# Smaller first loads, partial sums of two column blocks in one PSUM bank, and new planning estimates in a two-layer encoder trunk

## The chip, the cores and the metric

One Trainium2 chip, one core. The metric is the device time of one execution in microseconds (us), the median of several runs; lower is better. Matrix products run on PE (TensorE) and land in PSUM, which has eight banks of 512 fp32 columns per partition. DVE (VectorE), ACT (ScalarE) and POOL (GpSimd) do the elementwise work, and SP's queue issues nearly all DMAs.

## What is computed

Two layers over 256 tokens of width 1024, all in fp32. Each layer is: half a SwiGLU feed-forward (hidden width 2816), a mixer, cross attention to a memory of 256 tokens, and another half feed-forward. Layer 0's mixer is a differential attention beside a stick-breaking attention with one output projection; layer 1's is multi-head latent attention (MLA) with 16 heads.

```python
for layer in range(DEPTH):
    x = x + 0.5 * swiglu(rms_norm(x, ffn_norm[layer, 0]), w_gate, w_up, w_down)
    h = rms_norm(x, mix_norm[layer])
    x = x + (diff_stickbreak_mixer(h, ...) if layer % 2 == 0 else mla_mixer(h, ...))
    x = x + memory_cross_attention(rms_norm(x, xm_norm[layer]), rms_norm(mem, ...), ...)
    x = x + 0.5 * swiglu(rms_norm(x, ffn_norm[layer, 1]), w_gate, w_up, w_down)
```

## The kernel before

**Arithmetic.** Every fp32 product of weights is made of three matmuls on halves (mm3, L284 to L289): each operand is split into a rounded high part and a remainder, and high x high, low x high and high x low are summed in PSUM. Splitting costs one ACT cast (wh, L250) and one DVE subtraction (wl, L252; in the mixers the last 512 columns of a chunk go to POOL). The activations are kept feature by token (tile x, 8 blocks of 128 features by 256 tokens), also as pairs xh and xl.

**Weights.** They come in chunks of 1 MB in a fixed order (_plan). A chunk has one of two raw buffers (RAW), then one of three buffers of split halves (HL). A call of weight for chunk i issues loads and splits up to chunk i+2 (LOOK). The raw buffer comes free when its chunk is split, the split buffer when PE has used it.

**Start.** Before the first feed-forward, x and the first gate chunk are loaded in four parts each, and then the two halves of the first up chunk, the token-major copy of x (xtok, for the norm) and constants; the norm weights (gains) are loaded by SP's queue as the third DMA (L1483). fm_first runs the first gate chunk as its parts arrive. The norm's factor per token (rs) is computed by four ACT squares (L1497), and spread over the partitions by one matmul (spread) into rb, by which DVE scales the gate and up products when it empties their banks (L705, L713). For the first pair of chunks the PE order is gate 0, up 0, gate 1 with spread in its middle, and then up 1. Products take one of three banks tagged mm.

**PE's order in the mixers.** PE executes in exactly the order in which the program writes its instructions. In the mixers and cross attentions this order is made by a planner (run, L450): tasks are generators that yield what they need (a bank, an event, a chunk, a latency), planned times come from tables (EST_AB, EST_MLA, EST_X0, EST_X1) and from spend, and at each step the task with the lowest priority number of those that are ready goes on. The products and the output projection are one task of the lowest priority, the filler. If a real latency is longer than its estimate, PE stands and waits, with everything behind it. The other engines' orders are chosen by the framework's scheduler, also when the program is built.

**Output projection (out_g, L653).** The output has eight column blocks dt of 128 features. Its sum over the heads comes in groups, one for each event src at which heads are ready (four groups in the mixers, two in the cross attentions); one group of one block is two triples, six matmuls. A window of three blocks, each in its own mm bank, is taken through all groups, and then the other five blocks one by one. At a block's last group finish_dt adds the bank to x (DVE, L510), splits the result (ACT L481, DVE L482), squares it (ACT L522) and adds the square (POOL L530).

**MLA queries (L1312).** For each of 4 groups of heads and 2 halves of the tokens, queries scales the product, squares it, sums, takes one rsqrt (POOL, L467) and rotates in a scratch tile.

Of the kernel before, what the change touches and what calls it, by code (L numbers as in the profile page):

```python
# [53 lines left out]
SLOTS_MLA = (29, 11)  # L54
# [5 lines left out]
EST_X0 = {'scale': 3.59, 'rq': 1.14, 'psd': 1.46, 'sp': 2.8, 'p1': 4.06, 'p2': 0, 'o': 1.32, 'src': 8.83}  # L60
EST_X1 = {'scale': 2.31, 'rq': 1.14, 'psd': 1.46, 'sp': 2.8, 'p1': 3.39, 'p2': 0.0, 'o': 1.18, 'src': 8.83}
EST_AB = {'b': 1.33, 'va': 1.47, 'rot': 14.92, 'st1': 6.44, 'st2': 0.14, 'z': 1.55, 'sto': 2.4, 'src': 0.79, 'T': 0.74, 'sp': 3.0, 'pc': 8.7, 'pcT': 1.4, 'po': 4.35, 'oa': 8.7, 'srco': 1.25}
PRIO_MLA = [1, 2, 4.2, 3.9, 4.4, 2.3]
PRIO_AB = [1, 6.1, 4.1, 6.9, 6.9, 0.5]
EST_MLA = {'latd': 1.52, 'scale': 11.0, 'r': 1.8, 'kr': 4.06, 'pk': 2.4, 'pv': 1.23, 'v': 1.73, 'k': 6.43, 'kT': 0.9, 'q': 7.82, 'qT': 2.38, 'cs': 3.11, 'sp': 6.25, 'p1': 3.36, 'p2': 0.68, 'p3': 0.75, 'o': 0.58, 'src': 0.8}
MLA_ORDER = (('k', 0), ('kv', 0), ('kv', 1), ('q', 0), ('q', 1), ('k', 1), ('q', 2), ('q', 3), ('v', 0))
# [95 lines left out]
def trunk_kernel(ctx, tc, wflat, xT_d, xtok_d, memT_d, memtok_d, gains_d, rows_d, cst_d, out_d):  # L162
# [133 lines left out]
    nc.sync.dma_start(x[:, 0:2, :], xT_d[:, 0:2, :])  # L296
# [10 lines left out]
    for _ in range(13):  # L307
        PE.matmul(pw[:, 0:P], ones, ones, start=True, stop=True)
# [299 lines left out]
    def fm(w, xg, between=None, order=PLAIN):  # L608
        ps = ps_("mm")
# [43 lines left out]
    def out_g(keyf, nchunk, groups, gc):  # L653

        begin_phase()
        per = KT // nchunk
        ws, left, pss = {}, {c: per for c in range(nchunk)}, {}

        def part(dt, g):
            _, src, rows_ = groups[g]  # L660
            w = ws[dt // per]
            j = dt % per
            for i, k in enumerate(rows_):
                mm3(pss[dt][:, 0:S], (w[0][:, k, j * P:(j + 1) * P], w[1][:, k, j * P:(j + 1) * P]),
                    src[i], g == 0 and i == 0, g == len(groups) - 1 and i == len(rows_) - 1)
            if g == len(groups) - 1:
                left[dt // per] -= 1
                if not left[dt // per]:
                    done(keyf(dt // per))
                ps = pss.pop(dt)  # L670
                finish_dt(dt, gc, ps[:, 0:S])
                drop(ps, 0.8)

        nw = BANKS["mm"]
        for win in [tuple(range(nw))] + [(dt,) for dt in range(nw, KT)]:
            for g, (ev, _, _) in enumerate(groups):
                for dt in win:
                    yield dict(after=[ev], w=keyf(dt // per), mm=int(g == 0))
                    if dt // per not in ws:
                        ws[dt // per] = weight(keyf(dt // per), per * P)  # L680
                    if g == 0:
                        pss[dt] = take("mm")
                    part(dt, g)


    def ffn(l, j, gc, need_rb, mem=None):
# [4 lines left out]
        for f in range(FT // 2):  # L691
            pg = (fm_first(xg) if ("gate", l, j, f) == FIRST else
                  ahead or fm(weight(("gate", l, j, f), P), xg, order=PLAIN if f else EARLY))
            ahead = None
            if f == 0:
                if l == j == 0:
# [13 lines left out]
            if f:  # L710
                pu = fm(weight(("up", l, j, f), P), xg)
            u = al()
# [96 lines left out]
    def mem_k(l, c, events):  # L809
# [4 lines left out]
        def norm():  # L814
# [13 lines left out]
            yield dict(t=1, lat=7.0)  # L828
# [371 lines left out]
    def mixer_mla(gc):  # L1200
# [7 lines left out]
        rl, kk, kf, vt, kT, qf, rqs = {}, {}, {}, {}, {}, {}, {}  # L1208
# [88 lines left out]
        def turn_k(hf):  # L1297
            kT[hf] = []
            for g in range(4):
# [7 lines left out]
                drop(pt, 0.9)  # L1307
# [4 lines left out]
        def queries(n, t, ps):  # L1312

            yield dict(after=[ev["rcq"]])
            if t == 0:
                qf[n], rqs[n] = [], sl()
# [21 lines left out]
            rel(sq, tmp)  # L1338
# [137 lines left out]
    with arena(*SLOTS_FFN):  # L1476
        begin_phase()
        for h in range(4):
            if h:
                nc.sync.dma_start(x[:, 2 * h:2 * h + 2, :], xT_d[:, 2 * h:2 * h + 2, :])  # L1480
            split_w = issue_part(0, h, 4)
            if h == 0:
                nc.sync.dma_start(gains[:, 0:NG], gains_d)  # L1483
            for dt in (2 * h, 2 * h + 1):
# [8 lines left out]
        ss = sm()
        for q in range(4):
            xt = al()
            nc.sync.dma_start(xt, xtok_d[:, q // 2, (q % 2) * 512:(q % 2 + 1) * 512])
            A.activation(xt, xt, AF.Square, accum_out=ss[:, q:q + 1])  # L1497
            rel(xt)
        nc.sync.dma_start(cst, cst_d[:, 0:512])
        V.tensor_reduce(out=st.var, in_=ss[:, 0:4].rearrange("p (a b) -> p a b", b=2), axis=AX.X, op=ALU.add)  # L1500
        V.tensor_scalar(out=st.var, in0=st.var, scalar1=1.0 / D, scalar2=EPS, op0=ALU.mult, op1=ALU.add)
        rsqrt(st.var, 2, st.rs)
# [88 lines left out]
```

## Time and profile before

| what | us |
|---|---|
| median of 3 runs | 1087.91 (1087.11 to 1088.03) |
| profiled execution | 1090.49 |
| its span, first to last instruction | 1088.8 |
| PE busy in the span | 1065.9 |
| DVE, ACT, POOL busy | 769.4, 655.4, 192.5 |

The span is what the profile's rows cover. Starts are counted from its beginning. PE's matmuls are pipelined: a 128x256 matmul is shown with 0.28 us, but the next one starts 0.11 us after it, so time lost by PE is read from starts. The granted clock is TensorE's, as a share of 2.4 GHz; its other level is 1.2 GHz.

### The profile page before, as it was taken

What the parts mean: (1) busy time and instruction counts of PE and PEld (TensorE: products, weight loads), DVE (VectorE), ACT (ScalarE), POOL (GpSimd) and SP (SyncE); (2) the same over time, 40 slices, a digit from 0 to 9 for tenths busy, and PEclk for the clock granted to TensorE, in tenths of its full rate; (3) what the DMA queues carried; (4) which work ended last, traced back from release to release, by engine and by line L of the source; (5) the groups of instructions that cost most, each with busy time, mean ns of one, the idle gap of its engine ahead of it and who ended that gap; (6) DMA issues with size and microseconds to landing.
All of it is one profiled execution on the core that took longest, in us unless ns stands there. A gap on an engine that the chain in (4) does not pass through costs nothing.

```text
span 1088.8 us, 23382 instructions
## 1 busy us (share of the span) xinstructions
PE 1065.9 (98%) x9040; PEld 1046.5 (96%) x9040; DVE 769.4 (71%) x1866; ACT 655.4 (60%) x1775; POOL 192.5 (18%) x210
## 2 busy tenths in 40 slices
PE   9999999999989999999999999999989999999998
PEld 8899999998889999999999999999878999999998
DVE  5978766567867877776677777654678768777753
ACT  6666555576756765555565655555867567555542
POOL 1100001356245200000100000014861422000000
PEclk9999999999999999999999999999989999999999
DMA  8765555635346365545556555555342444555561
GB/s 291 248 223 209 195 198 186 195 116 161 111 126 199 107 219 179 211 177 198 185 194 219 193 215 179 202 186 161 110 131 64 144 145 167 205 190 198 184 220 63
DMA packets 50800, 193.36 MB, mean 178 GB/s; under 512 B 5760, under 2 KB 7552, under 8 KB 35584
## 3 DMA queue, kind: packets, MB, share of 16 engines
q1 hardware_dynamic: 50688, 191.86, 51.3%
q8 instruction: 71, 1.16, 0.4%
q14 instruction: 41, 0.34, 0.1%
HBM read 190.79 MB, written 1.05 MB: 176 GB/s over the span
## 4 chain that ended last, share of the span: by engine, by line
PE 87%; DVE 5%; ACT 2%; POOL 2%; DMA 2%; issue 1%; SPq 0%; DVEq 0%; ACTq 0%; POOLq 0%
PE mm L286 28%; PE mm L288 27%; PE mm L287 27%; DVE wl L252 2%; DMA wr<-wflat 2%; ACT slotf L754 1%; PE t L767 1%; POOL sm L467 1%; PE s L1422 1%; PE t L475 1%; PE s L892 0%; PE o L1455 0%; DVE sm L745 0%; ACT wh L250 0%; POOL sl L467 0%
## 5 line engine op out<-in xcount | busy, mean ns | idle before, releaser
L250 ACT CAST wh<-wr 128x256 fp32r<-128x256 f32 (+1 forms) x1216 | 441.2, 434 | 294.9 <-PE mm L287 237.8
L252 DVE TENSOR_TENSOR wl<-wr,wh 128x256 fp32r<-128x256 f32 (+1 forms) x1171 | 479.5, 464 | 122.1 <-ACT wh L250 117.1
L286 PE MATMUL mm<-xh,wh 128*128 128x256 f32 x1584 | 439.9, 278 | 3.8 <-DVE slotf L705 2.6
L288 PE MATMUL mm<-xh,wl 128*128 128x256 f32 x1584 | 437.6, 276 | 0.1
L287 PE MATMUL mm<-xl,wh 128*128 128x256 f32 x1584 | 437.4, 276 | 0.0
L286 PEld LDWEIGHTS mm<-xh,wh 128*128 128x128 f32 x1584 | 298.3, 188 | 5.0 <-issue 2.8
L287 PEld LDWEIGHTS mm<-xl,wh 128*128 128x128 f32 x1584 | 298.4, 188 | 0.6
L288 PEld LDWEIGHTS mm<-xh,wl 128*128 128x128 f32 x1584 | 298.1, 188 | 0.7 <-DVE wl L273 0.4
L286 PE MATMUL mm<-slotr,wh 128*128 128x256 f32 x896 | 247.6, 276 | 0.3 <-ACT slotr L481 0.3
L287 PE MATMUL mm<-slotr,wh 128*128 128x256 f32 x896 | 246.6, 275 | 0.4 <-DVE slotr L482 0.4
L288 PE MATMUL mm<-slotr,wl 128*128 128x256 f32 x896 | 246.5, 275 | 0.0
L286 PEld LDWEIGHTS mm<-slotr,wh 128*128 128x128 f32 x896 | 168.2, 188 | 1.0 <-ACT slotr L481 0.6
L287 PEld LDWEIGHTS mm<-slotr,wh 128*128 128x128 f32 x896 | 168.2, 188 | 0.7 <-DVE slotr L482 0.6
L288 PEld LDWEIGHTS mm<-slotr,wl 128*128 128x128 f32 x896 | 168.2, 188 | 0.0
L530 POOL TENSOR_TENSOR acc<-acc,sq 128x256 f32<-128x256 f32 x49 | 38.7, 790 | 455.0 <-ACT sq L522 452.9
L252 POOL TENSOR_TENSOR wl<-wr,wh 128x512 fp32r<-128x512 f32 x45 | 67.4, 1497 | 110.3 <-ACT wh L250 92.2
L713 DVE TENSOR_TENSOR slotf<-mm,rb 128x512 f32<-128x512 f32 x44 | 30.4, 690 | 59.4 <-PE mm L288 59.4
L481 ACT ACTIVATE xh<-x,gains 128x256 fp32r<-128x256 f32 x64 | 32.1, 507 | 29.8 <-DVE x L510 25.8
L705 DVE TENSOR_TENSOR slotf<-mm,rb 128x512 f32<-128x512 f32 x44 | 30.3, 689 | 23.4 <-PE mm L288 23.2
L754 ACT ACTIVATE slotf<-s,sm,sl 128x256 f32<-128x256 f32 (+1 forms) x64 | 32.8, 522 | 23.3 <-DVE sm L748 17.8
L510 DVE SCALAR_TENSOR_TENSOR x<-mm,x 128x256 f32<-128x256 f32 x64 | 26.7, 418 | 23.5 <-PE mm L288 23.3
L482 DVE SCALAR_TENSOR_TENSOR xl<-x,gains,xh 128x256 fp32r<-128x256 f32 x64 | 37.5, 590 | 5.3 <-ACT xh L481 5.2
(196 smaller groups left out, 1152.7 us busy)
## 6 DMA issues: line engine op xcount, KB each, us to landing
wr<-wflat SPq DMA_DIRECT2D x118, 1024.0 KB, 4.9
wr<-wflat SPq DMA_DIRECT2D x180, 256.0 KB, 3.9
wr<-wflat SPq DMA_DIRECT2D x16, 768.0 KB, 4.2
slotf<-memT SPq DMA_DIRECT2D x8, 256.0 KB, 3.4
x<-xT SPq DMA_DIRECT2D x4, 256.0 KB, 4.9
wr<-wflat SPq DMA_DIRECT2D x2, 512.0 KB, 8.2
slotf<-xtok SPq DMA_DIRECT2D x4, 256.0 KB, 7.8
slotf<-memtok SPq DMA_DIRECT2D x4, 256.0 KB, 3.6
```

The lines of the kernel that those rows point to most:

```text
L250: A.copy(hi[:, a:b], raw[:, a:b])
L252: e.tensor_tensor(out=lo[:, a:b], in0=raw[:, a:b], in1=hi[:, a:b].bitcast(F32), op=ALU.subtract)
L286: PE.matmul(out, a[0], b[0], start=first, stop=False, **kw)
L287: PE.matmul(out, a[0], b[1], start=False, stop=False, **kw)
L288: PE.matmul(out, a[1], b[0], start=False, stop=last, **kw)
L481: return (A.activation(hi, src, AF.Identity, scale=g), V.scalar_tensor_tensor(out=lo, in0=src, scalar=g, in1=hi.bitcast(F32), op0=ALU.mult ...
L482: V.scalar_tensor_tensor(out=lo, in0=src, scalar=g, in1=hi.bitcast(F32), op0=ALU.mult, op1=ALU.subtract))
L510: V.scalar_tensor_tensor(out=xd, in0=ps, scalar=factor, in1=xd, op0=ALU.mult, op1=ALU.add)
L530: G.tensor_tensor(out=st.acc, in0=st.acc, in1=sq, op=ALU.add)
L705: V.tensor_tensor(out=t.rearrange("p (a b) -> p a b", b=S), in0=pg.rearrange("p (a b) -> p a b", b=S), in1=rbb, op=ALU.mult)
L713: V.tensor_tensor(out=u.rearrange("p (a b) -> p a b", b=S), in0=pu.rearrange("p (a b) -> p a b", b=S), in1=rbb, op=ALU.mult)
L754: A.activation(p[:, i * w:(i + 1) * w], sps[:, i * w:(i + 1) * w], AF.Exp, bias=nb[:, i:i + 1], scale=r, accum_out=sums[:, i:i + 1])
```

## The change

1. Start: gains goes out first, by ScalarE's queue. x and the first gate chunk come in five parts (blocks 0, 1, 2-3, 4-5, 6-7). The token-major x and the norm move into first_norm, which the program now writes behind the first gate product; the constants are loaded in two pieces. PE's order is gate 0, up 0, gate 1, up 1 with spread in its middle, then gate 2; up 1 and gate 2 take the two banks tagged s, which the feed-forward doesn't use otherwise. setup (rope tables, masks) moves from the first pair to the fourth. 10 warming matmuls instead of 13.
2. out_g: two blocks share a bank, so the window has six blocks, and then one and one.
3. queries: one rsqrt for both halves of the tokens, scratch inside the tiles at hand, the rotation ahead of the sum.
4. Planner: new estimates, among them va, sp and srco (layer 0), k, kT, q, sp, p1, o and src (MLA), src of the cross attentions, 9 instead of 7 for a memory key; 0.115 instead of 0.109 per matmul; in MLA's product order the second key-value chunk moves behind two query chunks, and the last memory-value chunk ahead of the last query chunk. One more SBUF slot in MLA.

```diff
-EST_AB = {... 'va': 1.47, ... 'sp': 3.0, ... 'srco': 1.25}
+EST_AB = {... 'va': 2.8, ... 'sp': 4.4, ... 'srco': 2.2}
-EST_MLA = {... 'k': 6.43, 'kT': 0.9, 'q': 7.82, 'qT': 2.38, 'cs': 3.11, 'sp': 6.25, 'p1': 3.36, 'p2': 0.68, ... 'o': 0.58, 'src': 0.8}
+EST_MLA = {... 'k': 9.0, 'kT': 1.5, 'q': 8.0, 'qT': 3.0, 'cs': 2.0, 'sp': 4.6, 'p1': 4.4, 'p2': 1.2, ... 'o': 2.2, 'src': 1.6}
-MLA_ORDER = (('k', 0), ('kv', 0), ('kv', 1), ('q', 0), ('q', 1), ('k', 1), ('q', 2), ('q', 3), ('v', 0))
+MLA_ORDER = (('k', 0), ('kv', 0), ('q', 0), ('q', 1), ('kv', 1), ('k', 1), ('q', 2), ('v', 0), ('q', 3))
...
-    nc.sync.dma_start(x[:, 0:2, :], xT_d[:, 0:2, :])
+    nc.scalar.dma_start(gains[:, 0:NG], gains_d)
+    nc.sync.dma_start(x[:, 0:1, :], xT_d[:, 0:1, :])
...
             for i, k in enumerate(rows_):
-                mm3(pss[dt][:, 0:S], (w[0][:, k, j * P:(j + 1) * P], w[1][:, k, j * P:(j + 1) * P]),
-                    src[i], g == 0 and i == 0, g == len(groups) - 1 and i == len(rows_) - 1)
+                mm3(ps[:, dt % 2 * S:dt % 2 * S + S], (w[0][:, k, j * P:(j + 1) * P], w[1][:, k, j * P:(j + 1) * P]),
+                    src[i], g == i == dt % 2 == 0, g == len(groups) - 1 and i == len(rows_) - 1,
+                    skip_group_check=True)
...
-                ps = pss.pop(dt)
-                finish_dt(dt, gc, ps[:, 0:S])
-                drop(ps, 0.8)
+                finish_dt(dt, gc, ps[:, dt % 2 * S:dt % 2 * S + S])
+                if dt % 2:
+                    drop(ps, 0.8)
 
-        nw = BANKS["mm"]
+        nw = 2 * BANKS["mm"]
...
                 if first_:
+                    first_norm()
                     pu = fm(weight(("up", l, j, f), P), xg)
-                    ahead = fm(weight(("gate", l, j, 1), P), xg, tick)
-                    setup()
+                    ahead = (fm(weight(("gate", l, j, 1), P), xg),
+                             fm(weight(("up", l, j, 1), P), xg, tick, tag="s"))
...
+            if t:
+                v = qv[n][:, 0:8]
+                V.tensor_scalar(out=v, in0=v, scalar1=96 * EPS, scalar2=None, op0=ALU.add)
+                rsqrt(v, 8, rqs[n])
```

## Rows read from the trace of the kernel before

**Rows 1.** The page, part 1: busy us (share of the span) x instructions.
```profile
PE 1065.9 (98%) x9040; PEld 1046.5 (96%) x9040; DVE 769.4 (71%) x1866; ACT 655.4 (60%) x1775; POOL 192.5 (18%) x210
```
**Rows 2.** Stretches: length, busy us of each engine, clock, DMA share, GB/s.
```profile
0.00:40.00 40.00, 35.07 (x245) 33.49 (x246) 28.09 (x78) 26.84 (x76) 6.20 (x20) 0.96 0.82 279
...
200.00:273.00 73.00, 71.17 (x607) 68.24 (x605) 47.90 (x74) 47.19 (x102) 39.07 (x39) 1.00 0.47 150
273.00:345.00 72.00, 67.13 (x580) 65.05 (x579) 53.84 (x115) 45.27 (x109) 30.11 (x25) 1.00 0.45 143
345.00:370.00 25.00, 24.43 (x183) 23.07 (x182) 19.60 (x49) 18.08 (x50) 5.22 (x6) 1.00 0.33 122
...
733.00:800.00 67.00, 62.10 (x443) 57.79 (x443) 39.09 (x85) 44.10 (x86) 46.00 (x50) 0.97 0.41 132
800.00:847.00 47.00, 44.98 (x330) 39.95 (x330) 40.72 (x115) 31.95 (x94) 13.01 (x16) 0.97 0.27 87
```
**Rows 3.** Waits of PE over the span: us in total, times, longest.
```profile
PE s L1422 <- DVE slotf L1409: 2.6, 1, 2.6
PE t L767 <- DVE slotf L827: 2.5, 2, 2.2
PE s L323 <- ACT slotf L754: 2.3, 3, 1.0
PE t L767 <- ACT slotf L1305: 1.4, 1, 1.4
...
PE o L1079 <- issue: 0.9, 1, 0.9
PE o L1079 <- ACT slotf L991: 0.9, 1, 0.9
```
**Rows 4.** Timeline of PE, 20 to 32 us: start, us, operation, idle before.
```profile
20.88 0.39 PE L286 MATMUL mm<-xh,wh 128*128 128x256 f32 x1 [1.17 <-ACT wh L250]
...
27.10 0.28 PE L288 MATMUL mm<-xh,wl 128*128 128x256 f32 x1
30.02 0.35 PE L286 MATMUL mm<-xh,wh 128*128 128x256 f32 x1 [2.64 <-DVE slotf L705]
...
31.16 0.41 PE L286 MATMUL mm<-xh,wh 128*128 128x256 f32 x1
```
**Rows 5.** Timeline of SP, ACT and DVE, 6 to 30 us.
```profile
6.78 3.25 SPq L1496 DMA_DIRECT2D slotf<-xtok  x4
...
13.03 3.84 SPq L248 DMA_DIRECT2D wr<-wflat  x2
...
20.42 2.56 ACT L250 CAST wh<-wr 128x256 fp32r<-128x256 f32 x8 [2.04 <-DMA wr<-wflat]
...
24.31 4.03 DVE L252 TENSOR_TENSOR wl<-wr,wh 128x256 fp32r<-128x256 f32 x8 [0.68 <-ACT wh L250]
...
29.19 0.68 DVE L705 TENSOR_TENSOR slotf<-mm,rb 128x512 f32<-128x512 f32 x1
```
**Rows 6.** The POOL rsqrt of L467 in the MLA stage, 773 to 818 us.
```profile
L467 POOL TENSOR_TENSOR sl<-sm,small x7: 1006/1377/1583, 785.9 to 814.6; 128x4 f32<-128x4 f32 x7
```
**Rows 7.** Timeline of ACT, 757 to 761 us.
```profile
757.74 0.60 ACT L1218 ACTIVATE slotf<-mm 128x512 f32<-128x512 f32 x1 [0.46 <-DVE slotr L482]
759.92 0.84 ACT L818 ACTIVATE slotf<-mm,small 128x256 f32<-128x256 f32 x2 [1.58 <-PE mm L288]
```
**Rows 8.** Timeline of PE and DVE, the output projection of layer 0's mixer.
```profile
317.91 0.28 PE L288 MATMUL mm<-slotr,wl 128*128 128x256 f32 x1
...
319.27 0.28 PE L288 MATMUL mm<-slotr,wl 128*128 128x256 f32 x1
...
318.22 0.42 DVE L510 SCALAR_TENSOR_TENSOR x<-mm,x 128x256 f32<-128x256 f32 x1 [2.35 <-PE mm L288]
...
322.67 0.41 DVE L510 SCALAR_TENSOR_TENSOR x<-mm,x 128x256 f32<-128x256 f32 x1
...
333.69 0.41 DVE L510 SCALAR_TENSOR_TENSOR x<-mm,x 128x256 f32<-128x256 f32 x1
```

More of the change, by code (lines that the diff above doesn't have):

```diff
@@ L306, in trunk_kernel @@
     pw = ps_("o")
-    for _ in range(13):
+    for _ in range(10):
         PE.matmul(pw[:, 0:P], ones, ones, start=True, stop=True)
@@ L605, in trunk_kernel, with fm @@
     PLAIN = [(j, k) for j in range(2) for k in range(KT)]
-    def fm(w, xg, between=None, order=PLAIN):
-        ps = ps_("mm")
+    def fm(w, xg, between=None, order=PLAIN, tag="mm"):
+        ps = ps_(tag)
         for j, k in order:
@@ L677, in out_g, with first_norm @@
                 for dt in win:
-                    yield dict(after=[ev], w=keyf(dt // per), mm=int(g == 0))
+                    yield dict(after=[ev], w=keyf(dt // per), mm=int(g == 0 and dt % 2 == 0))
                     if dt // per not in ws:
                         ws[dt // per] = weight(keyf(dt // per), per * P)
-                    if g == 0:
-                        pss[dt] = take("mm")
+                    if g == 0 and dt % 2 == 0:
+                        pss[dt // 2] = take("mm")
                     part(dt, g)
+    def first_norm():
+        ss = sm()
+        for q in range(4):
+            xt = al()
+            nc.sync.dma_start(xt, xtok_d[:, q // 2, (q % 2) * 512:(q % 2 + 1) * 512])
+            A.activation(xt, xt, AF.Square, accum_out=ss[:, q:q + 1])
+            rel(xt)
+        nc.sync.dma_start(ident, cst_d[:, C_ID:C_ID + P])
+        with tc.high_priority():
+            V.tensor_reduce(out=st.var, in_=ss[:, 0:4].rearrange("p (a b) -> p a b", b=2), axis=AX.X, op=ALU.add)
+            V.tensor_scalar(out=st.var, in0=st.var, scalar1=1.0 / D, scalar2=EPS, op0=ALU.mult, op1=ALU.add)
+            rsqrt(st.var, 2, st.rs)
     def ffn(l, j, gc, need_rb, mem=None):
@@ L691, in ffn @@
         for f in range(FT // 2):
[L692 to L693 removed]
+            first_ = l == j == 0
+            pu = None
+            if ahead and f:
+                pg, pu = ahead
+            elif first_ and f == 0:
+                pg = fm_first(xg)
+            else:
+                pg = fm(weight(("gate", l, j, f), P), xg, order=PLAIN if f else EARLY,
+                        tag="s" if first_ and f == 2 else "mm")
             ahead = None
             if f == 0:
[L696 removed]
+                if first_:
+                    first_norm()
                     pu = fm(weight(("up", l, j, f), P), xg)
[L698 to L699 removed]
+                    ahead = (fm(weight(("gate", l, j, 1), P), xg),
+                             fm(weight(("up", l, j, 1), P), xg, tick, tag="s"))
                 else:
@@ L709, in ffn @@
             rel(t)
-            if f:
+            if pu is None:
                 pu = fm(weight(("up", l, j, f), P), xg)
+            if first_ and f == 3:
+                setup()
             u = al()
@@ L1477, in trunk_kernel @@
         begin_phase()
[L1478 to L1484, printed above, removed]
+        for k0, k1 in ((0, 1), (1, 2), (2, 4), (4, 6), (6, 8)):
+            if k0:
+                nc.sync.dma_start(x[:, k0:k1, :], xT_d[:, k0:k1, :])
+            split_w = issue_part(0, k0 * 256, k1 * 256)
+            for dt in range(k0, k1):
                 for made in finish_dt(dt, G_FFN):
@@ L1488, in trunk_kernel @@
         for h in range(2):
-            issue_part(1, h, 2)()
+            issue_part(1, h * 1024, (h + 1) * 1024)()
         st.xg = st.nxt
         st.rs, st.var, st.rb = sl()[:, 0:2], sl()[:, 0:2], T("rb", [P, S], 1)
[L1493 to L1502, printed above, removed]
         st.todo = [spread]
```

40 lines of the change are left out of this document (19 added, 21 removed).

## Prediction

> **What bounds the kernel now.** I read the page's busy times first: PE is busy for 1065.9 of 1088.8 us [rows 1], so the end is PE's work plus PE's waits, and no other engine is near the bound over the span. Then the stretches: PE's idle time sits in the start (40.00 - 35.07 = 4.9 us, 1.1 of it before anything can run), in layer 0's mixer (1.83 + 4.87 = 6.7), in MLA (4.90 + 2.02 = 6.9) and, 0.6 each, in the first cross attention [rows 2] and in the second. The granted clock is below 1 in the start and in MLA. A mean of 0.96 over 40 us, with 0.5 and 1 as the only levels, is 3.2 us at 1.2 GHz, of which half, 1.6 us, is lost; 0.97 over 67 and 47 us loses 2.0 and 1.4 us [rows 2]. In the start the fall follows the 2.64 us wait: from 31.16 us a matmul takes 0.41 us instead of 0.28 [rows 4].
>
> Third, the waits by name [rows 3]: nearly all are PE standing at an instruction whose data is late by 1 to 2.6 us, in an order fixed when the program was written. Idle time understates them. Before the 2.64 us wait PE's starts are 27.10 and 30.02, 2.92 apart instead of 0.11, and the next matmuls start slower: a wait costs about 0.25 us more than its idle row [rows 4]. With some 6 such waits in layer 0's mixer and 10 in MLA, what can be won is about 8.2 us and, with the clock, 6.9 + 2.5 + 3.4 = 12.8 us.
>
> **Start.** PE stood twice. At 20.88 it waited 1.17 for the cast of gate 1's weights, which waited 2.04 for their DMA [rows 5]; SP issued the four xtok loads at 6.78 and that chunk only at 13.03, so 1 MB lay ahead of it. Now the program writes xtok behind the chunk. If SP's queue follows, gate 1 lands in time: -1.4. If the scheduler still puts xtok first, only the 0.19 MB of constants that are split off go away, 0.7 us at the 279 GB/s of the stretch [rows 2]: -0.7. At 30.02 up 1 waited for a bank, held by gate 0, whose reading (L705, 29.19) stood on DVE behind the eight wl of 24.31 to 28.34 [rows 5]. Up 1's weights were there from 24.7. With two s banks, up 1 and gate 2 need none of these three; the first bank is wanted again only by up 2, five chunks of 48 x 0.113 = 5.4 us after gate 0 begins, past 33 us, and L705 can run from about 28.5: -2.8 and the 1.6 us of clock. The norm's chain moves later, but spread now stands in the middle of up 1, at about 27.5; four squares end by 23 to 25 and the sum, rsqrt and DVE need 1.5. The first product may begin 1.2 us earlier, but its last weight part still comes with the same 2 MB, so I take 0 for that (bounds 0 and -1.2). setup, on DVE and POOL in the fourth pair, is hidden: DVE is busy for 28 of the first 40 us. gains costs ACT one issue while it has no data. Sum **-5.8** (bounds -4 and -7).
>
> **Layer 0's mixer.** The re-derived estimates are close to old value plus the wait in the rows: va 1.47 to 2.8 where L1079 waited 0.9 for L991, sp 3.0 to 4.4 for L323's waits, 9 for the 2.2 us at L767 behind L827 [rows 3]. The planner puts filler there instead, if it has some. The two at L1079, 0.9 each and 2.3 with their 0.25, have products behind them and simply go. Late in the stage only the output projection is left; the three more blocks of the window give 3 x 2 early groups x 0.68 us = 4.1 us of filler. I take **-5.5** of 8.2 (bounds -1 and -8): blocks 4 and 5 need a third chunk, which the planner may meet too early.
>
> **MLA.** queries issues 4 rsqrt on POOL instead of 8: 4 x 1.38 = 5.5 us off an engine busy for 46 of 67 us there [rows 2, 6], in a stretch that holds the waits of 2.6 and 1.4 us [rows 3]. Filler: 3 x 3 x 0.68 = 6.1 us. With the clock's 3.4 I take **-9** of 12.8 (bounds -3 and -12). Query chunk 3 is now last, so its heads' chain has no memory product behind it; that is why I don't take all. **Cross attentions**: their src falls from 8.83 to 2.0, which lets the first group run as filler: **-1** together (0 and -2).
>
> **The shared bank.** Here the change adds a wait. Block 1's last matmuls write the bank from which DVE has yet to read block 0 (L510). Does PE wait for a reader of other columns? No row shows that direction. Two rows are near it. ACT stood idle for 1.58 us with half a bank ready, until PE's last matmul into the other half; and it stood 0.46 us before reading a bank that DVE was still reading, with no data between the two [rows 7]. So the program orders any two engines on one bank, and I take the wait as certain to 9 in 10. The Trainium skill, page PSUM — Partial Sum Buffer, section PSUM bank collisions raise a hardware error, says that PSUM is to be guarded by bank and quadrant, not by address, since TensorE's write and another engine's read of other columns collide too; by that rule the price below is due in full, without it nothing. The rows agree with it as far as they go.
>
> Price: block 0's last matmul starts at 317.91, DVE reads from 318.22 to 318.64, and PE starts 0.15 after a release (29.87 to 30.02), at 318.79 instead of 318.02, which is 0.11 after 317.91; with a slower first matmul 0.85 [rows 4, 5, 8]. There are 4 pairs in each of 4 projections: 16 x 0.85 = **+13.6** (bounds 0 and 16). What stands behind the waiting matmul is all of PE. To this comes how late DVE is. Block 3 ended on PE at 319.27 + 24 x 0.113 + 0.28 = 322.26, and was read at 322.67, 0.4 late; block 6 ended, 72 matmuls later, at 330.4 and was read at 333.69, 3.3 late, behind wl of later chunks [rows 8]. That lateness cost nothing before, as no matmul wanted the bank. I take the nearer row, 0.4 us, for blocks 4 and 6, as PE's own waits thin the reads out: 8 x 0.4 = **+3.2** (bounds 0 and 13). The fourth chunk's split buffer now comes free only four blocks, 2.7 us of matmuls, ahead of its use, where the planner's own constant for making a chunk ready is 4.41; the waits of two pairs, 1.7, cover the difference.
>
> **Sum.** -5.8 - 5.5 - 9 - 1 + 13.6 + 3.2 = -4.5 us. Against the profiled execution's own 1090.5 that is 1086.0; it lies 2.6 above the median of the runs, so on the median's scale 1083.4.
>
> **Rivals.**
> *Late reads (slower).* The read of block 6 stays behind the wl of the next chunks in DVE's fixed order, as at 333.69. Then block 7 waits 3.3 us more in each mixer and, by an estimate in the middle between 0.4 and 3.3, 2 more in each cross attention: 10.6 instead of 1.6 for these four, net +4.5, 1092.4. It decides from some 1.2 us of lateness per projection upwards. For it: the row itself. Against: six blocks now end in one go, and their reads were prompt in the window.
> *The waits move on.* The chains of the mixers, not the estimates, set their ends, and half of the 14.5 us stays: net +2.8, 1090.7. For it: DVE is busy for 40.7 of 47 us late in MLA [rows 2]. Against: POOL's relief and the filler.
> *No bank wait (the change does not add what I say).* Different columns go past each other: -21.3, 1066.6. Only the direction not shown speaks for it.
>
> **Numbers.** Forecast 0.48, late reads 0.24, waits move on 0.14, no bank wait 0.14. 0.2% is 2.2 us, about what a measurement of this kernel can tell from no change. The forecast's own bounds reach about 6 us to either side; I count 0.42 of its 0.48 as faster and 0.06 as within, 0.02 of late reads and 0.06 of the waits that move as within. Faster 0.42 + 0.14 = 0.56, within 0.14, slower 0.30. The range takes in the slower rivals with some 3 us of their own, up to 1096, and reaches down to 1072, short of the case without bank waits, which with a tail above is the 2 in 10 left out. The likeliest case alone has 1077 to 1090.
>
> **What would show it.** In the changed profile: no wait between gate 1 and up 2 and clock 1.0 from 20 to 40 us, with the fifth chunk starting about 6 us sooner (start right); 16 waits of PE in out_g for DVE's x, at least 0.6 idle each (bank wait right), those of block 7 longest (late reads); PE idle in the mixers outside the projections below 5 us together, and no half clock in MLA (estimates right). It would be wrong if no PE wait names DVE x, if gate 0 itself ends over 1 us sooner, or if MLA's waits reappear under other names.

## The result, and the profile after

The changed kernel takes 1116.7 us (median of 4 runs, 1115.2 to 1117.5), the kernel before 1087.5 beside it: a ratio of 1.026, with an interval of 1.0243 to 1.0277. It is 29 us slower, where 4.5 us less were forecast.

The page of the kernel after, its span and part 1 (busy us, share of the span, instructions):

```profile
span 1115.2 us, 23353 instructions
PE 1074.2 (96%) x9034; PEld 1051.1 (94%) x9034; DVE 777.0 (70%) x1862; ACT 657.6 (59%) x1775; POOL 190.1 (17%) x206
```

Against [rows 1] PE's idle time rose from 22.9 to 41.0 us, and its busy time rose by 8.3 with six instructions fewer, so its matmuls ran slower too. Where, the stretches say. Stretches of the kernel after, with the columns of [rows 2]: the start, late in layer 0's mixer, the first cross attention, and MLA:

```profile
0.00:40.00 40.00, 36.78 (x277) 35.48 (x278) 26.14 (x71) 26.60 (x74) 2.06 (x9) 0.96 0.79 270
261.00:333.60 72.60, 65.65 (x564) 62.72 (x563) 50.86 (x109) 44.50 (x108) 24.70 (x22) 1.00 0.41 131
333.60:379.00 45.40, 42.04 (x321) 39.62 (x321) 33.52 (x74) 27.29 (x72) 14.21 (x15) 1.00 0.35 117
739.00:888.10 149.10, 130.83 (x919) 119.35 (x918) 99.60 (x219) 87.18 (x205) 63.84 (x69) 0.94 0.32 107
```

PE does 32 instructions more in the 40 us of the start. In MLA idle time and a lower clock come together: 149.1 - 130.8 = 18.3 us idle at a mean clock of 0.94. The waits of PE in the kernel after (us in total, times, longest; the same statement has other line numbers in each kernel, a few lines apart):

```profile
PE mm L285 <- DVE x L511: 15.7, 16, 2.3
PE s L323 <- ACT slotf L784: 3.4, 2, 2.7
PE t L797 <- ACT slotf L1335: 2.9, 1, 2.9
PE t L797 <- DVE slotf L1440: 2.6, 1, 2.6
PE o L1486 <- DVE slotf L805: 2.2, 2, 1.1
...
PE t L476 <- POOL acc L531: 1.6, 2, 0.8
```

The first line answers no line of [rows 3]: it is the shared bank, 16 waits. The next four lie in MLA, but for 0.7 us of the first of them, and the last shown is the norm of a feed-forward, which waits 0.8 twice for POOL's sum of squares (L531) behind an output projection.

To put each difference in its stage I measured a stage from the last addition to x of one (the last DVE write of x in its projection) to that of the next. In us; a layer's first and second feed-forward are FF1 and FF2:

| kernel | start and FF1 | layer 0's mixer | cross 0 | FF2 | MLA | cross 1 | FF2 of layer 1 |
|---|---|---|---|---|---|---|---|
| before | 195.56 | 139.99 | 39.69 | 178.70 | 133.08 | 39.52 | 178.70 |
| after | 191.26 | 141.96 | 45.49 | 179.53 | 149.09 | 44.54 | 179.50 |
| a_single | 191.15 | 136.40 | 42.41 | 178.70 | 145.50 | 40.37 | 178.70 |
| b_start | 191.47 | 140.01 | 39.74 | 178.70 | 133.11 | 39.53 | 178.70 |
| c_pairs | 194.30 | 146.70 | 44.53 | 179.52 | 138.76 | 44.32 | 179.52 |
| d_oldorder | 191.19 | 136.39 | 42.33 | 178.70 | 142.73 | 40.32 | 178.68 |
| e_oldest | 190.72 | 136.33 | 42.34 | 178.70 | 131.93 | 40.34 | 178.67 |
| g_apart | 190.96 | 142.73 | 41.56 | 180.51 | 148.24 | 39.03 | 180.51 |
| h_abest | 191.58 | 140.77 | 39.76 | 178.70 | 132.70 | 39.50 | 178.70 |
| i_spend | 190.26 | 141.15 | 39.71 | 178.67 | 134.24 | 39.52 | 178.67 |
| m_k | 190.83 | 136.33 | 42.27 | 178.67 | 136.42 | 40.34 | 178.70 |
| n_sp | 190.81 | 136.35 | 42.31 | 178.67 | 135.90 | 40.35 | 178.70 |
| p_best | 190.17 | 136.37 | 39.73 | 178.67 | 132.28 | 39.56 | 178.70 |

Layer 1's first feed-forward takes 180.80 in each.

### The profile page after: what moved, and what is told of

Its sections match the earlier page's. It is cut to its first block, busy times and chain, and to the rows that moved or that the text cites. A ratio compares the mean times of both kernels' runs of the same rounds, so it can differ in the third digit from the quotient of the medians.

```text
span 1115.2 us, 23353 instructions
## 1 busy us (share of the span) xinstructions
PE 1074.2 (96%) x9034; PEld 1051.1 (94%) x9034; DVE 777.0 (70%) x1862; ACT 657.6 (59%) x1775; POOL 190.1 (17%) x206
## 4 chain that ended last, share of the span: by engine, by line
PE 82%; DVE 8%; ACT 3%; POOL 2%; issue 2%; DMA 2%; SPq 0%; DVEq 0%; ACTq 0%; POOLq 0%
PE mm L285 26%; PE mm L286 26%; PE mm L287 25%; DVE wl L252 2%; DMA wr<-wflat 2%; ACT slotf L784 1%; DVE x L511 1%; PE t L797 1%; ACT wh L250 1%; POOL sm L468 1%; DVE xl L483 1%; DVE sm L775 1%; PE t L476 1%; DVE slotf L789 0%; PE o L941 0%
## 5 line engine op out<-in xcount | busy, mean ns | idle before, releaser
L252 DVE TENSOR_TENSOR wl<-wr,wh 128x256 fp32r<-128x256 f32 (+1 forms) x1171 | 484.9, 471 | 128.1 <-ACT wh L250 119.5
L285 PE MATMUL mm<-xh,wh 128*128 128x256 f32 x1552 | 430.6, 277 | 2.0 <-ACT wh L271 2.0
L287 PE MATMUL mm<-xh,wl 128*128 128x256 f32 x1552 | 428.6, 276 | 0.0
L286 PE MATMUL mm<-xl,wh 128*128 128x256 f32 x1552 | 428.4, 276 | 0.0
L285 PEld LDWEIGHTS mm<-xh,wh 128*128 128x128 f32 x1552 | 292.5, 188 | 2.7 <-ACT wh L271 2.2
L287 PEld LDWEIGHTS mm<-xh,wl 128*128 128x128 f32 x1552 | 292.2, 188 | 0.5 <-DVE wl L272 0.3
L286 PEld LDWEIGHTS mm<-xl,wh 128*128 128x128 f32 x1552 | 292.3, 188 | 0.2
L285 PE MATMUL mm<-slotr,wh 128*128 128x256 f32 x896 | 251.0, 280 | 16.5 <-DVE x L511 15.7
L531 POOL TENSOR_TENSOR acc<-acc,sq 128x256 f32<-128x256 f32 x49 | 45.5, 928 | 451.5 <-ACT sq L523 448.6
L252 POOL TENSOR_TENSOR wl<-wr,wh 128x512 fp32r<-128x512 f32 x45 | 64.9, 1442 | 145.5 <-ACT wh L250 133.3
```

Source lines behind the costliest of these rows:

```text
L252: e.tensor_tensor(out=lo[:, a:b], in0=raw[:, a:b], in1=hi[:, a:b].bitcast(F32), op=ALU.subtract)
L531: G.tensor_tensor(out=st.acc, in0=st.acc, in1=sq, op=ALU.add)
```

## The experiments

### The parts: a_single, b_start, c_pairs, d_oldorder

a_single is the kernel after with out_g as before, one block a bank and a window of three:

```diff
-        nw = 2 * BANKS["mm"]
+        nw = BANKS["mm"]
...
-                finish_dt(dt, gc, ps[:, dt % 2 * S:dt % 2 * S + S])
-                if dt % 2:
-                    drop(ps, 0.8)
+                finish_dt(dt, gc, ps[:, 0:S])
+                drop(ps, 0.8)
```

> The changed kernel with its old output projection (one column block a bank, window of three), all else as changed. Theory 1, the bank waits: the 16 waits of PE for DVE's reading of the other block cost 18.3 us counted from PE's starts (6.1 in each mixer, 3.0 in each cross attention), and go: about 1098 us. Theory 2, the window: the six-block window also spoils the planner's order in MLA and the cross attentions, which lost some 10 and 5 us beyond those waits: then up to 30 us go, about 1086. Theory 3, the wait for the bank is a symptom (PE would wait for the next chunk of weights anyway): at most 5 us go, 1112.

Measured: 1098.9 us, ratio 1.0098 (1.0074 to 1.0121). So the pairs cost 1116.7 - 1098.9 = 17.8 us, and without them the change still loses 11. The table says where: MLA +12.4 against before, cross attentions +2.7 and +0.9, start -4.4, layer 0's mixer -3.6.

b_start is the kernel before with the new start alone (issue_part, first_norm, setup, the two s banks, gains on ScalarE's queue, 10 warming matmuls, and the one more SBUF slot in MLA):

```diff
-    nc.sync.dma_start(x[:, 0:2, :], xT_d[:, 0:2, :])
+    nc.scalar.dma_start(gains[:, 0:NG], gains_d)
+    nc.sync.dma_start(x[:, 0:1, :], xT_d[:, 0:1, :])
...
-                    ahead = fm(weight(("gate", l, j, 1), P), xg, tick)
+                    ahead = (fm(weight(("gate", l, j, 1), P), xg),
+                             fm(weight(("up", l, j, 1), P), xg, tick, tag="s"))
```

> The kernel before with the change's start alone (finer loads, gains by ScalarE's queue, the norm behind the first product, two s banks). Theory: the 4.3 us by which the first feed-forward ended sooner in the changed kernel are all of it and last to the end: 1083.2 us. Rival: the later stages give it back, as they are paced by weights: 1087.

Measured: 1086.35 us, ratio 0.9989 (0.9978 to 0.9999). The stage is 4.1 us shorter than in the trace of before, the median only 1.1. The profiled execution of before lay 2.6 to 3 us above its median, and c_pairs, with the old start again, took 194.30 in this stage, 1.3 less than before; against that the gain is 2.8. The later stages take the same time as in before's trace, within 0.05 us each, so the rival's way of losing it, later stages that give it back, is not what the traces show. By the median the start is worth 1.1 us (0.1 to 2.4 by the interval), and why the profiles show more stays open.

c_pairs is the kernel before with the new out_g alone:

```diff
-        nw = BANKS["mm"]
+        nw = 2 * BANKS["mm"]
...
-                    if g == 0:
-                        pss[dt] = take("mm")
+                    if g == 0 and dt % 2 == 0:
+                        pss[dt // 2] = take("mm")
```

> The kernel before with the two-block banks alone. Theory 1, bank waits: +18 us, less up to 4 that six blocks of filler give back in each mixer: 1098 to 1106 us. Theory 3, symptom: no more than 1092.

Measured: 1111.0 us, ratio 1.021 (1.0185 to 1.0234), 23.5 us more, with the same line among the waits of PE in c_pairs:

```profile
PE mm L286 <- DVE x L510: 15.7, 16, 2.3
```

That is above the 1098 to 1106 expected. The four stages with a projection lose 6.7 + 4.8 + 5.7 + 4.8 = 22.0 us by the table and the feed-forwards behind them 1.6. Counted from PE's starts the 16 waits are 18.4 us; of the other 5 the feed-forwards have 1.6, and no run isolates the rest. The six-block window's filler won nothing that can be seen: the waits before the projections all stand, 6.3 us in layer 0's mixer and 6.8 in MLA, where the kernel before has 6.6 and 6.9.

d_oldorder is a_single with the product order of before in MLA:

```diff
-MLA_ORDER = (('k', 0), ('kv', 0), ('q', 0), ('q', 1), ('kv', 1), ('k', 1), ('q', 2), ('v', 0), ('q', 3))
+MLA_ORDER = (('k', 0), ('kv', 0), ('kv', 1), ('q', 0), ('q', 1), ('k', 1), ('q', 2), ('q', 3), ('v', 0))
```

> As a_single, with MLA's product order as before. If the new order (second key-value chunk later, last query chunk last) made MLA longer: 8 to 10 us less than a_single. If the new estimates did: the same as a_single within 2 us.

Measured: 1095.6 us, ratio 1.007 (1.0053 to 1.0087), MLA 142.73. That is 3.3 us less than a_single, between the two expectations: the order is 2.8 of MLA's 12.4 us, and not the main part. It was tried only beside the new estimates.

### Estimates, queries, spacing: e_oldest, f_oldq, g_apart, h_abest

e_oldest is d_oldorder with MLA's old estimates:

```diff
-EST_MLA = {... 'pk': 1.6, ... 'k': 9.0, 'kT': 1.5, 'q': 8.0, 'qT': 3.0, 'cs': 2.0, 'sp': 4.6, 'p1': 4.4, 'p2': 1.2, ... 'o': 2.2, 'src': 1.6}
+EST_MLA = {... 'pk': 2.4, ... 'k': 6.43, 'kT': 0.9, 'q': 7.82, 'qT': 2.38, 'cs': 3.11, 'sp': 6.25, 'p1': 3.36, 'p2': 0.68, ... 'o': 0.58, 'src': 0.8}
...
-                drop(pt, 1.5)
+                drop(pt, 0.9)
```

> As d_oldorder, with MLA's old estimates too (table and the release of a key transpose's bank). MLA took 142.7 us in d_oldorder and 133.1 in the kernel before. Theory: the new estimates make MLA longer; back to 133 to 135 there, about 1087 us in all. Rival: the rewritten queries, or 0.115 us per matmul, did it: MLA stays at 141 to 143, 1095.

Measured: 1084.7 us, ratio 0.9973 (0.996 to 0.9987), MLA 131.93. The estimates are 10.8 us of MLA's loss, and without them the kernel is faster than before.

f_oldq is d_oldorder with queries as before (eight rsqrt of 128x4 instead of four of 128x8, a scratch tile of its own):

```diff
-            if t:
-                v = qv[n][:, 0:8]
-                V.tensor_scalar(out=v, in0=v, scalar1=96 * EPS, scalar2=None, op0=ALU.add)
-                rsqrt(v, 8, rqs[n])
...
+            rsqrt(v, 4, rqs[n][:, t * 4:(t + 1) * 4])
```

> As d_oldorder, with the old queries (8 rsqrt, scratch tile, no rotation ahead of the sum), new estimates kept. If the new queries relieve POOL as forecast: MLA 2 to 5 us longer than d_oldorder's 142.7. If they are what makes MLA longer (the sum now stands behind the rotation): MLA shorter by over 3 us.

Measured: 1096.3 us and 142.97 in MLA, beside 1095.6 and 142.73: the rewritten queries are worth nothing here. POOL's rsqrt of the queries in MLA, by the form, first d_oldorder and then f_oldq (busy us, mean ns):

```profile
L468 POOL TENSOR_TENSOR sl<-sm,small 128x8 f32<-128x8 f32 x4 | 9.9, 2479 | 9.4 <-DVE sm L1363 7.0 <-DVE sm L774 2.4
```

```profile
L468 POOL TENSOR_TENSOR sl<-sm,small 128x4 f32<-128x4 f32 x8 | 10.0, 1249 | 10.5 <-DVE sm L1351 10.5
```

Four of twice the width take as long as eight here, so POOL got no relief. In the kernel after the four take 7.5 us, where the kernel before has 9.9 for its eight.

g_apart is the kernel after with the last group of the window taken in the order 0, 2, 4, 1, 3, 5, so that other blocks stand between the two of a bank:

```diff
-                for dt in win:
+                last = g == len(groups) - 1 and len(win) > 1
+                for dt in (win[0::2] + win[1::2] if last else win):
```

> The changed kernel, with the last group taken through the window in the order 0, 2, 4, 1, 3, 5, so that two other blocks stand on PE between the two of a bank. If PE waits for the reading of the neighbour block in the same bank: the three waits of the window shrink to nearly nothing in the cross attentions (2.3 of 3.0 us each; the wait of block 7 for block 6 stays), and in the mixers up to 3.6 each, less what the fourth chunk, whose buffer now comes free two blocks later, costs. 4 to 10 us less than the changed kernel's 1116.7. If PE waits for something else at these places (the engine behind, the weights): no change, 1115 to 1118.

Measured: 1109.7 us, ratio 1.0198 (1.0181 to 1.0215), 7 us below after. The waits of PE in g_apart:

```profile
PE mm L287 <- POOL wl L252: 3.4, 2, 2.0
...
PE mm L285 <- DVE x L511: 3.3, 4, 1.1
PE mm L287 <- DVE wl L252: 2.8, 2, 1.5
...
PE mm L285 <- ACT wh L250: 1.4, 1, 1.4
```

The waits for x fell from 15.7 to 3.3 us, and the cross attentions give back 3.9 and 5.5, of which the feed-forwards behind them lose 1.0 each. In the mixers splits of weights take their place, 3.4 + 2.8 + 1.4 us: the new order keeps the first chunk's split buffer until the fourth block instead of the second, and the fourth chunk, which needs it, is late. Layer 0's mixer is even longer, 142.7.

h_abest is b_start with layer 0's new estimates and 9 for a memory key:

```diff
-EST_AB = {... 'va': 1.47, ... 'sp': 3.0, ... 'srco': 1.25}
+EST_AB = {... 'va': 2.8, ... 'sp': 4.4, ... 'srco': 2.2}
...
-            yield dict(t=1, lat=7.0)
+            yield dict(t=1, lat=9.0)
```

> The start alone, plus the new estimates of layer 0's mixer and 9 us for the memory keys. That stage took 140.0 us before and 136.4 in a_single. Theory: these estimates are the gain: stage 136 to 137, 3.5 us less than b_start's 1086.4, about 1083. Rival: the gain came with 0.115 us per matmul: stage stays at 139 to 140.

Measured: 1086.1 us, 140.77 in the mixer: alone, these estimates win nothing.

### Which estimates: i_spend, k_front, l_back, m_k, n_sp, o_pk

i_spend is b_start with 0.115 for 0.109:

```diff
-        spend(3 * 0.109 * b[0].shape[-1] / 256)
+        spend(3 * 0.115 * b[0].shape[-1] / 256)
```

> The kernel before with the new start, and one constant of the plan changed: what a product of three matmuls counts in the planner, 0.115 us instead of 0.109. Theory (the constant, and not the estimates, made layer 0's mixer shorter): its stage goes from 140.0 to about 136.4 us, and the time to about 1082.8. Rival (both are needed): it stays at 139 to 140.8. For the cross attentions: if the constant is what lengthened the first one, its stage goes from 39.7 to 42.4; if the estimates did, it stays at 39.7. MLA's stage, 133.1 before, should lie between 131.9 and 133.1.

Measured: 1086.9 us, ratio 0.9984 (0.9973 to 0.9996), 141.15 in layer 0's mixer and 39.71 in the first cross attention. The theory fell: the mixer's 136.4 needs the estimates and the constant together. And the constant alone does not lengthen the cross attention. MLA took 134.24, above the 133.1 expected, which is less than one profile leaves uncertain there (last section).

j_oldx, despite its label, is e_oldest itself:

> e_oldest, to be measured again beside the other three: old product order and old estimates in MLA, new estimates in the cross attentions and layer 0's mixer, 0.115. The same 1084.7 us as before is expected (1082 to 1088), with 42.3, 40.3 and 131.9 us in the two cross attentions and MLA.

Measured: 1085.7 us, MLA 130.69.

k_front and l_back are e_oldest with one half each of MLA's new estimates:

```diff
-EST_MLA = {... 'pk': 2.4, ... 'k': 6.43, 'kT': 0.9, ...}
+EST_MLA = {... 'pk': 1.6, ... 'k': 9.0, 'kT': 1.5, ...}
```

> e_oldest with the new estimates of the key side of MLA alone: pk 1.6, k 9.0, kT 1.5 and the bank of the keys' transposes counted as taken for 1.5 us. With all new estimates MLA took 142.7 us, with the old ones 131.9. Theory (the key chain's estimates are what spoils the order: key products are planned 2.6 us later, and everything behind them too): 138 to 143 us. Rival (the estimates of the memory chain spoil it): 131.5 to 133.

```diff
-EST_MLA = {... 'cs': 3.11, 'sp': 6.25, 'p1': 3.36, 'p2': 0.68, ... 'o': 0.58, 'src': 0.8}
+EST_MLA = {... 'cs': 2.0, 'sp': 4.6, 'p1': 4.4, 'p2': 1.2, ... 'o': 2.2, 'src': 1.6}
```

> e_oldest with the new estimates of MLA's memory chain alone: cs 2.0, sp 4.6, p1 4.4, p2 1.2, o 2.2, src 1.6. Theory (the key chain's estimates spoil the order): 131 to 133 us in MLA, and the time within 1.5 us of e_oldest's. Rival (the memory chain's estimates do: sp, falling from 6.25 to 4.6, lets PE come too early to products whose data are late): 138 to 143 us, and a time 6 to 11 us above e_oldest's.

Measured: 1088.3 and 1089.1 us, 136.24 and 137.13 in MLA. Neither theory nor rival was right alone: each half costs 3 to 4 us of time. The next three runs split them: k alone, sp alone, and pk with kT.

```diff
-EST_MLA = {... 'k': 6.43, ...}
+EST_MLA = {... 'k': 9.0, ...}
```

> e_oldest with one new estimate alone, k 9.0 instead of 6.43 (when the planner counts a key chunk as ready). The key side's three new estimates with the longer bank time of the transposes gave 136.2 us in MLA, the old ones 130.7 to 131.9. Theory (k is what moves three query chunks ahead of the transposes of the keys, whose copies then stand on ACT behind the queries' work): 135 to 138 us, with a wait of over 4 us at the transposes for the copy of the keys. Rival (the earlier release of the product banks, pk, or the longer transposes, kT, do it): 130.5 to 132.5.

```diff
-EST_MLA = {... 'sp': 6.25, ...}
+EST_MLA = {... 'sp': 4.6, ...}
```

> e_oldest with one new estimate alone, sp 4.6 instead of 6.25 (how long the planner counts a bank of scores as taken). The memory chain's six new estimates gave 137.1 us in MLA and waits of 6.9 us at the masks for ACT's exponentials, where e_oldest has 0.9. Theory (sp lets PE come to a bank that ACT still reads): 135 to 138 us, and at least 4 us of waits at the masks. Rival (the later products, p1, p2 and o, or cs, do it): 130.5 to 132.5 us and at most 1.5 us of such waits.

```diff
-EST_MLA = {... 'pk': 2.4, ... 'kT': 0.9, ...}
+EST_MLA = {... 'pk': 1.6, ... 'kT': 1.5, ...}
```

> The rest of the key side: e_oldest with pk 1.6 and kT 1.5 and the bank of the transposes counted as taken for 1.5 us, and k left at 6.43. Theory of m_k (k does it): 130.5 to 132.5 us in MLA. Rival: 135 to 138.

Measured: m_k 1089.1 us, n_sp 1088.4, o_pk 1085.2. m_k has the same instructions in the same order on all engines as k_front, and o_pk as e_oldest and j_oldx. So k is all of the key side and pk and kT are nothing, and there are 30 executions of e_oldest's program, median 1085.2: k costs 3 to 4 us, sp 3.2. All six of the memory chain cost 3.9 (l_back), so sp is most of them. The two halves make 7 to 8 of the 10.9 us by which d_oldorder's median lies above e_oldest's; whether the rest comes from q and qT, which no run changed alone, or from the halves acting on each other is not shown. o_pk's 134.52 in MLA missed both ranges for another reason, shown in the last section, on the clock.

How k does it is seen in the waits of PE in MLA, first e_oldest and then m_k:

```profile
PE t L793 <- DVE slotf L785: 3.2, 1, 3.2
PE t L793 <- DVE slotf L853: 2.5, 1, 2.5
PE t L793 <- POOL slotf L1316: 2.4, 1, 2.4
PE s L323 <- ACT slotf L780: 0.2, 1, 0.2
```

```profile
PE t L793 <- ACT slotf L1331: 4.3, 1, 4.3
PE t L793 <- DVE slotf L785: 3.2, 1, 3.2
PE t L793 <- DVE slotf L853: 1.2, 1, 1.2
```

The estimate did what it was for: the 2.4 us at the transposes of the keys, for POOL's part of them (L1316), are gone. In their place the planner had put query products. Their work went to ACT, DVE and POOL ahead of the keys' copies. The timeline of m_k, POOL, DVE, ACT and PE, start, us, operation and idle before:

```profile
775.84 1.73 POOL L252 TENSOR_TENSOR wl<-wr,wh 128x512 fp32r<-128x512 f32 x1
777.52 2.25 POOL L1355 TENSOR_TENSOR slotf<-slotf,mqb 128x64 f32<-128x64 f32 x4
...
775.54 3.30 DVE L252 TENSOR_TENSOR wl<-wr,wh 128x512 fp32r<-128x512 f32 x3
...
780.97 0.55 DVE L1359 TENSOR_REDUCE sm<-slotf 128x4 f32<-128x384 f32 x1
...
781.62 0.62 ACT L250 CAST wh<-wr 128x512 fp32r<-128x512 f32 x1 [4.72 <-DVE sm L1359]
782.14 0.52 ACT L1348 ACTIVATE slotf<-slotf 128x384 f32<-128x384 f32 x1
782.57 1.24 ACT L1331 ACTIVATE slotf<-t,small 96x512 f32<-96x512 f32 x2
...
783.29 1.94 PE L793 MATMUL t<-cst,slotf 128*96 128x128 f32 x8 [4.26 <-ACT slotf L1331]
```

POOL rotates queries (L1355) behind a wl, DVE reduces them (L1359) behind three wl and that, ACT stands 4.72 us until DVE's reduction ends at 781.52, and the copies of the keys' transposes (L1331), for which PE waits 4.26 us, stand behind it in ACT's order. But PE's idle time in m_k's MLA is only 1.0 us above e_oldest's, 9.3 against 8.3 us; its busy time rose by 3.5 us for the same products, at a clock of 0.95 instead of 0.99 (rows in the last section). So in these two profiles most of the 4.5 us is the clock. The last section shows that as much can come and go between executions of one program; the 3 to 4 us are read from the medians, and how they divide between idle time and clock is not shown.

With sp at 4.6 the waits stand at the masks, ahead of the scores. The timeline of n_sp, PE and ACT:

```profile
788.46 1.05 PE L1449 MATMUL s<-slotf,slotf 96*128 96x128 f32 x8
...
794.87 0.33 PE L323 MATMUL s<-mk,mq 128*128 128x128 f32 x1 [1.43 <-ACT slotf L780]
...
792.95 0.46 ACT L780 ACTIVATE slotf<-s,sm,sl 128x128 f32<-128x128 f32 x1 [1.51 <-DVE sm L774]
...
794.27 0.46 ACT L780 ACTIVATE slotf<-s,sm,sl 128x128 f32<-128x128 f32 x1
```

The first scores (L1449 at 788.46) end about 789.5, and the last exponential that reads their bank (794.27 + 0.46) at 794.7, over 5 us later; a bank counted as taken for 4.6 brings PE too early, one of 6.25 does not. All three such waits of the run are 3.3 us, below the 4 expected. In MLA they are 2.5 us where e_oldest has 0.2, and n_sp's MLA idles 2.8 us more than e_oldest's (rows in the last section). In d_oldorder's MLA both waits stand together, 4.3 us for L1331 and 3.1 us at L323.

### A version that beats both: p_best

p_best is e_oldest with the old estimates of the cross attentions:

```diff
-EST_X0 = {... 'o': 1.6, 'src': 2.0}
-EST_X1 = {... 'o': 1.6, 'src': 2.0}
+EST_X0 = {... 'o': 1.32, 'src': 8.83}
+EST_X1 = {... 'o': 1.18, 'src': 8.83}
```

> e_oldest with the old estimates of the cross attentions too: of the change there stay the start, the queries' new chain, the constant 0.115 and layer 0's mixer with its new estimates. Theory (the cross attentions' new src 2.0 and o 1.6 lengthened them, since the constant alone left the first at 39.7): 39.7 and 39.5 us instead of 42.3 and 40.3, and a time 3.4 us below e_oldest's, about 1081 to 1082, which would beat both kernels. Rival (new estimates are needed with the constant): 42 and 40 us, 1084 to 1086.

Measured: 1083.0 us, ratio 0.9959 (0.9946 to 0.9971), with 39.73 and 39.56 in the cross attentions as the theory had it; 2.2 us below e_oldest's program instead of 3.4. It beats both kernels, the one before by 0.4%. What the old estimates took away is seen in e_oldest's first cross attention, in the waits of PE from 327 to 370 us:

```profile
PE mm L286 <- DVE slotr L488: 0.9, 2, 0.6
PE mm L285 <- ACT slotr L487: 0.7, 1, 0.7
```

With the new estimates the output projection's first 18 products come ahead of the last heads' matmuls, and before ACT and DVE have split their operand (L487, L488); in p_best all of them follow in one go, without these waits. src and o were taken back together, so which of them does it is argued from src's fall from 8.83 to 2.0, not shown.

## Why the prediction was wrong, step by step

**The shared bank** was right. All 16 waits are there. The timeline of PE and DVE in the kernel after, output projection of layer 0's mixer:

```profile
316.91 0.39 PE L285 MATMUL mm<-slotr,wh 128*128 128x256 f32 x1 [0.52 <-DVE x L511]
319.59 0.39 PE L285 MATMUL mm<-slotr,wh 128*128 128x256 f32 x1 [1.01 <-DVE x L511]
322.91 0.39 PE L285 MATMUL mm<-slotr,wh 128*128 128x256 f32 x1 [1.64 <-DVE x L511]
326.35 0.28 PE L287 MATMUL mm<-slotr,wl 128*128 128x256 f32 x1
328.95 0.39 PE L285 MATMUL mm<-slotr,wh 128*128 128x256 f32 x1 [2.33 <-DVE x L511]
...
316.43 0.42 DVE L511 SCALAR_TENSOR_TENSOR x<-mm,x 128x256 f32<-128x256 f32 x1 [10.35 <-PE mm L287]
...
325.65 2.92 DVE L252 TENSOR_TENSOR wl<-wr,wh 128x512 fp32r<-128x512 f32 x2
328.49 0.41 DVE L511 SCALAR_TENSOR_TENSOR x<-mm,x 128x256 f32<-128x256 f32 x1
```

From start to start the waits of this projection cost 0.68, 1.18, 1.80 and 2.49 us (the last is 328.95 - 326.35 - 0.11), and all 16 of them 18.3, where 13.6 + 3.2 = 16.8 was forecast; a_single against after gives 17.8. c_pairs against before gives 23.5, so the agreement owes something to luck. The least, 0.68, lies below the 0.85: PE starts 0.06 us after the read ends, not 0.15. The last is the rival of the late reads in its place and with its cause, two wl, 2.92 us together, ahead of the read, but at 1.8 us over the least and only in the mixers (block 7 waits 0.7 from start to start in each cross attention). So it took 3.6 of the 10.6 us that I gave it. The Trainium skill, page PSUM — Partial Sum Buffer, section PSUM bank collisions raise a hardware error, asks for guards by bank and quadrant and not by address; the order of the program agrees, at 0.68 us and more for each guard. No run here shows what would happen without one. What I missed is 0.8 us in each of two feed-forwards, where the norm waits for POOL.

**Start**: -4.3 in the trace, within my bounds of -4 and -7, but only -1.1 by b_start's median, outside them, and by a path that I had partly wrong. The stalls between gate 1 and up 2 went as said, but for 0.18 us. SP's queue in the kernel after did follow the program:

```profile
13.78 0.33 SPq L248 DMA_DIRECT2D wr<-wflat  x1
14.15 2.07 SPq L695 DMA_DIRECT2D slotf<-xtok  x4
```

But the first product, for which I took 0, got a new wait. In the timeline of PE in the kernel after:

```profile
9.24 0.39 PE L285 MATMUL mm<-xh,wh 128*128 128x256 f32 x1 [1.98 <-ACT wh L271]
```

So gate 0's last matmul starts 1.3 us later than before, at 15.20 instead of 13.89. The clock went as said in the second 20 us, 1.00 where it was 0.91, and fell in the first, behind this wait:

```profile
0.00:20.00 20.00, 16.96 (x110) 16.07 (x111) 10.54 (x30) 11.66 (x30) 0.59 (x7) 0.91 0.72 233
20.00:40.00 20.00, 19.82 (x170) 19.41 (x169) 15.61 (x42) 14.93 (x45) 1.47 (x2) 1.00 0.85 308
```

The mean of the 40 us stayed at 0.96, so the 1.6 us of clock were not won in this execution; in e_oldest, with the same start, both halves are at 1.00.

**Layer 0's mixer**: -3.6 instead of -5.5, within the bounds of -1 and -8. The waits that I named went (2.2, 0.9 and 0.9 us are no longer in the list). But a_single has this gain without the six-block window, so the 4.1 us of filler that I counted were not its reason. And h_abest and i_spend show what I left out: the estimates do it only together with the constant 0.115, which no step of mine priced.

**MLA is the step that failed**: "-9 of 12.8 (bounds -3 and -12)" measured +12.4 with one block a bank. Of that the new estimates are +10.8 and the new product order +2.8; the rest of the change is -1.2. My step summed three gains, POOL's relief, filler and the clock, and put the new estimates and the order at nothing. None of the three came as counted. The relief of 4 x 1.38 = 5.5 us counted the four rsqrt that stay as being as short as those of 128x4; they are of 128x8, so POOL won 2.4 us in the kernel after and nothing in d_oldorder, and undoing the rewrite changed nothing (f_oldq). The filler of 6.1 us was that of the six-block window, and with it 6.8 of 6.9 us of waits stayed (c_pairs). The clock did not rise from 0.97: it was 0.96 in a_single and 0.94 in the kernel after. And the estimates had two effects that I did not ask for. A larger k puts query products ahead of the keys' transposes, and their work on ACT, DVE and POOL delays the keys (m_k). A smaller sp, 4.6 instead of 6.25, brings PE to a bank sooner; [rows 3] had no wait in MLA that this could cure, and 0.4 us at L323 there that it could only lengthen (n_sp). cs fell too, from 3.11 to 2.0, but was not run alone. The rival in which the waits move on came nearest, since it let the chains and not the estimates set the ends; its price stopped at half of the gain lost, and had no room for a loss.

**Cross attentions**: "-1 together (0 and -2)" measured +2.7 and +0.9. That the first group then runs as filler was true; that its operand is then late was the cost (p_best, which took back src and o together).

**No bank wait** fell in c_pairs. In sum, by the stages: -4.3 start, -3.6 layer 0's mixer, +12.4 MLA, +3.6 cross attentions and +18.0 pairs give +26.1; the profiled spans differ by 26.4. The medians differ by 29.2, as the profiled execution of before lay 3.0 us above its median and that of after 0.2. Without the failed steps of MLA and the cross attentions my terms would have given +5.5 for the forecast, still slower: the gains there were the whole case for faster.

## What to carry to other kernels

A planner's estimate is an order, not a measurement: raising one to the latency seen removes that wait and puts other work in front, whose followers on the other engines' queues can delay the same chain by more. Change estimates one at a time and keep those that shorten the stage; here layer 0's did, with a second constant, and MLA's and the cross attentions' did not. And two sums that share a PSUM bank make PE wait for each read of the first, so they should end far apart, and even that moves the wait when, as in g_apart, it holds a weight buffer longer.

## What the runs showed of the hardware that I had not expected

Three executions of one program differ in MLA by 3.8 us, most of it by the clock. The stretch of MLA, columns as in [rows 2], in e_oldest, in j_oldx and in o_pk, which have the same instructions in the same order:

```profile
728.90:860.80 131.90, 123.61 (x939) 114.92 (x938) 97.58 (x218) 86.60 (x205) 65.88 (x70) 0.99 0.38 120
```

```profile
729.90:860.60 130.70, 122.79 (x940) 113.92 (x939) 96.53 (x219) 86.63 (x205) 66.87 (x70) 1.00 0.38 121
```

```profile
729.30:863.80 134.50, 126.18 (x939) 116.90 (x938) 97.82 (x218) 86.80 (x205) 65.88 (x70) 0.96 0.37 118
```

PE is idle for 8.3, 7.9 and 8.3 us in them; the granted clock is 0.99, 1.00 and 0.96. Its levels are 1.2 and 2.4 GHz, so a mean of 0.96 over 134.5 us is 10.8 us at the lower one, of which at most half, 5.4, is lost: time at the lower level in which PE stands idle costs nothing. What the rows show is 3.4 us, by which PE's busy time in o_pk exceeds j_oldx's for the same products. The stretch in m_k, n_sp and d_oldorder:

```profile
729.00:865.40 136.40, 127.12 (x939) 117.89 (x938) 94.94 (x219) 86.73 (x205) 66.12 (x70) 0.95 0.36 116
```

```profile
728.90:864.80 135.90, 124.83 (x938) 114.93 (x937) 98.76 (x219) 87.10 (x206) 65.39 (x70) 0.99 0.36 117
```

```profile
729.40:872.10 142.70, 129.36 (x939) 120.38 (x938) 97.73 (x219) 86.73 (x205) 67.40 (x70) 0.94 0.33 111
```

n_sp idles 11.1 us at 0.99, so 2.8 of its 4.0 us over e_oldest are idle time. m_k's 4.5 are 1.0 of idle and 3.5 of busy time. d_oldorder's 10.8 are 5.0 of idle and 5.7 of busy time: more than half of what MLA's estimates cost there is PE running the same products more slowly, at a mean clock of 0.94, in a stage with 5.0 us more of waits. A stage's length in one profile is therefore uncertain by some 4 us in this stretch, and it was the 10 or more executions of each program, not the stage, that told e_oldest from m_k and n_sp.
